# Half of the normed tokens parked in DRAM, and S5 spread one step per projection part, in a Hymba-style layer on one core

## The chip, the core and the metric

The kernel runs on one core of a Trainium2 chip. The core has a matrix engine (PE, with its weight loads PEld), a vector engine (DVE), an activation engine (ACT), a general engine (POOL) and an engine that issues DMAs (SP). Each takes its own instructions strictly in order; semaphores make one wait for another. The metric is the device time of one execution in microseconds. Before the change the median of three runs is 1477.52 us (1474.14 to 1479.11).

## The reference, cut

```python
mod = silu(c) @ w_ada + b_ada;  shift, scale, gate = split(mod, 3)
h = rmsnorm(x, norm_g) * (1 + scale) + shift          # 2048 prompt + 64 sample tokens, D = 1024
u, z_s, q, k, v, z_a, f_logit = split(h @ w_in)       # 512 columns each, 8 logits
y_ssm = Re(C scan(A, B u)) + D u                      # S5: 32 groups of 16 channels, 64 complex states
y_ssm = gelu(y_ssm);  y_ssm = y_ssm * sigmoid(y_ssm @ w_glu + b_glu) * silu(z_s)
q, k = rmsnorm per head;  logf = log_sigmoid(f_logit + b_f);  cum = cumsum(logf)
o = softmax(q k^T / 8 + cum_q - cum_k, causal) v      # 8 heads x 64; the sample also sees a cache of 512
y = x + gate * (concat(y_ssm, o * silu(z_a)) @ w_out)
```

Outputs are y, k, v, logf and the last S5 states, for the prompt and for the sample, all in float32.

## The kernel before

**Stages.** `body` (L1491) writes the program: the adaLN vectors (`Ada`, 1 MB chunks of w_ada; chunks 0 to 3 are shift and scale, 4 and 5 the gate), the projection (`InProj`) with the S5 branch (`S5`) woven into it, the GLU, attention (`Attn`) and the output projection (`Out`). A tile scheduler orders each engine's instructions ahead of time from this program and from what depends on what; at run time nothing is reordered. SP issues all DMAs, up to eight in flight.

**Projection.** The tokens are four groups of 512 (the last with the 64 sample tokens). `norm(g)` (L437) loads a group's x, transposes it on PE, applies shift and scale on ACT (hf, L460) and splits it on DVE into two float32r tiles hi and lo, so that a product takes three matmuls (`mm3`, L313: hi·whi, hi·wlo, lo·whi). The rings for hi and lo hold two groups: one half of the tokens. So the projection runs twice over the weights, for half (0, 1), then for half (2, 3). For each half there are 12 parts of 256 columns: u0, u1, then ten parts: k0, k1, v0, v1, q0, q1 and four gate parts. `weights` (L464) loads a part's 1 MB in two transfers into wst; ACT casts to whi, DVE takes the rest to wlo, in rings of 5.

`natural` (L482) makes u, v, k and q with the tokens on the partitions: a tile is 128 tokens x 256 columns, 24 matmuls. ACT evicts u and v (L500). A k or q tile goes ACT square (L507), DVE reduce (L508), DVE and POOL for the reciprocal root (L294, L295), DVE twice for the product (L511, L512). u0 also makes the forget logits (lf). `gates` (L517) makes the two gates transposed, in matmuls of 512 columns; ACT takes tanh (L534), DVE multiplies (L535), and th is stored in z_d. The tiles of the projection use three PSUM banks (2, 3, 4); two serve transposes, three S5.

**S5.** It needs u of all tokens. `setup` (L581) makes the powers of the discretised state matrix by a long chain of small DVE operations (128x32 and the like, L611). 16 steps of two groups follow. `consts(s)` (L774) makes a step's matrices on DVE (lin, btt, ca), PE and POOL; `load` (L837) brings u (un, ug); `run` (L856) does the PE matmuls us·bt, the scan on DVE (L883 to L904) and aa; `outs` (L907) does the matmuls tm·us and ca·aa, then GELU on ACT; `store` (L850) writes ys_d. A call of `s5_step` does run(s), outs(s-1) and consts(s+1), so 17 calls do all; `final` (L937) writes the states.

**Order before.** Half (0, 1): norm, u0, u1, parts; the gate chunks of w_ada ahead of part 1, setup and the first two consts ahead of part 3. Half (2, 3): norm, u0, 8 steps, u1, then parts with 3 steps after each; ahead of part 7 what is left of S5, `logf` (L538, cumulative sums of the logits) and the attention's bias. In the program:

```python
GATE_AT = 1      # w_ada chunks 4 and 5 ahead of this part of half (0, 1)
SETUP_AT = 3     # S5 setup ahead of this part of half (0, 1)
LOGF_AT = 7      # logf, bias ahead of this part of half (2, 3)
S5_STEPS = 3     # calls of s5_step after each part of half (2, 3)
```

Of the kernel before, what the change touches and what calls it, by code (L numbers as in the profile page):

```python
# [17 lines left out]
P = 128  # L18
# [25 lines left out]


GATE_AT = 1
SETUP_AT = 3
LOGF_AT = 7
S5_STEPS = 3
# [116 lines left out]
def Step(tc, a, o, ctx):  # L166
# [44 lines left out]
    cb_d = dram.tile([H, 21 * P], F32, name="cb_d")  # L211

# [187 lines left out]
class InProj:  # L400
# [62 lines left out]

    def weights(self, c0, n):  # L464
# [105 lines left out]
class S5:  # L570
# [10 lines left out]
    def setup(self):  # L581
# [5 lines left out]
        def tl(name, shape, p=sb):  # L587
            return p.tile([P] + shape, F32, name=name)
# [19 lines left out]
        S.activation(dt, dt, AF.Exp)  # L608
# [13 lines left out]
        S.activation(mag, lam, AF.Exp)  # L622
        self.r8 = tl("r8", [G], cp)
        S.activation(self.r8, lam, AF.Exp, scale=float(TC))
# [282 lines left out]
    def outs(self, s, f):  # L907
# [6 lines left out]
        for i, (c, r) in enumerate(cts):  # L914
# [11 lines left out]
            if r == P:  # L926
                S.activation(dst, py[:r].rearrange("c g (t q) -> c g t q", q=PG), AF.Gelu_apprx_tanh)
            else:
                for g in range(GS):
                    S.activation(dst[:, g], py[32 * g:32 * g + r, 0].rearrange("c (t q) -> c t q", q=PG),  # L930
                                 AF.Gelu_apprx_tanh)
# [22 lines left out]
class Attn:  # L954
# [260 lines left out]
    def scores(self, tile, kd, t):  # L1215
# [24 lines left out]
        j = i % 2 if whole and not (i == tile.nb - 1 and acc[1] is None) else 0  # L1240
# [41 lines left out]
    def run(self, out):  # L1282
# [10 lines left out]
        for i, (hp, qt) in enumerate(self.order):  # L1293
            self.cur = i
            while i not in self.ready:
# [11 lines left out]
                                   given=[False, False], n=0, nb=len(blocks), po=None)  # L1307
# [26 lines left out]
            if tile.acc[1] is not None:  # L1334
                e.PL.tensor_tensor(tile.acc[0][:, :, :nq], tile.acc[0][:, :, :nq], tile.acc[1][:, :, :nq], op=ALU.add)
# [155 lines left out]
def body(tc, a, o):  # L1491
    with ExitStack() as top:
# [35 lines left out]
        for half in ((0, 1), (2, 3)):  # L1528
            if half[0]:
                for g in half:  # L1530
                    ip.norm(g)
                ip.natural("u", 0, half)
            if half[0]:
                for _ in range(8):
                    s5_step()
            ip.natural("u", 1, half)
            for part in range(10):
                if not half[0] and part == GATE_AT:
                    for n in (4, 5):
                        ad.chunk(n)  # L1540
                if not half[0] and part == SETUP_AT:
                    s5.setup()
                    kc.update({0: s5.consts(0), 1: s5.consts(1)})
                if half[0] and part == LOGF_AT:
                    while done[0] <= NSET:
                        s5_step()
                    s5.final()
                    e.table("natural_log_exp_and_others", AF.Tanh, AF.Gelu_apprx_tanh)
                    ip.logf(s5.ps)
                    e.table("exp_and_others", AF.Exp, AF.Ln)  # L1550
                    at = Attn(e)
                    at.bias(s5.ps)
                if part < 6:
                    ip.natural("kvq"[part // 2], part % 2, half)
                else:
                    ip.gates(part - 6, half)
                if half[0]:
                    for _ in range(S5_STEPS):
                        s5_step()
# [4 lines left out]
        with ExitStack() as es:  # L1564
# [3 lines left out]
            e.table("natural_log_exp_and_others", AF.Tanh)  # L1568
# [32 lines left out]
```

## Time and profile before

| | |
|---|---|
| median of three runs | 1477.52 us |
| the profiled execution | 1474.66 us |
| its span (first to last instruction) | 1472.6 us |
| mean granted PE clock | 0.981 |
| instructions | 26341 |

By PE's matmul counts the parts end at these times (us from the start of the span):

| half | u0 | u1 | k0 | k1 | v0 | v1 | q0 | q1 | four gate parts |
|---|---|---|---|---|---|---|---|---|---|
| (0, 1) | 69.0 | 91.7 | 114.5 | 141.6 | 169.7 | 199.5 | 226.0 | 249.4 | 338.3 |
| (2, 3) | 371.9 | 410.5 | 448.8 | 496.5 | 537.8 | 578.4 | 622.7 | 665.3 | 772.7 |

The page cuts the span into 40 slices of 36.8 us; a digit is the busy share in tenths, PEclk the granted clock of PE:

```profile
PE   5899999999988999889999999999999897999998
DVE  3726886235689987996313777786886887333331
PEclk9999999999999999999999979999999999999999
```

The projection takes slices 1 to 21. In a row of the view by groups stand line, engine, operation, result and operands with their shape and count, then busy us and the mean ns of one, then the idle time before them and what ended it. In the view of PE's waits a row says who waited for whom, the us in total, how often, and the longest.

### The profile page before, as it was taken

The page shows a single profiled execution, that of the slowest core. Times are in us where ns is not written, and L with a number is a line of the kernel's source. Part 1 is how long each engine was busy: PE and PEld are TensorE (multiplying, and loading weights), DVE is VectorE, ACT ScalarE, POOL GpSimd, SP SyncE. Part 2 cuts the span into 40 slices and gives each one's busy share as a digit, 9 for nine tenths or more (in the row PEclk, how much of TensorE's full clock was granted, in tenths as well). Part 3 has the DMA queues.
Part 4 walks back from the last instruction along what each step waited for, and adds up shares of the span by engine and source line. Part 5 has one row for each costly group of instructions (what it writes and reads, how often), then busy time and mean ns, then how long its engine had stood idle before and what let it go on. Part 6 is the DMA issues. An engine that isn't in the chain of part 4 may idle for free.

```text
span 1472.6 us, 26341 instructions
## 1 busy us (share of the span) xinstructions
PE 1391.7 (95%) x9824; PEld 1092.2 (74%) x9824; DVE 912.3 (62%) x2398; ACT 538.6 (37%) x1132; POOL 485.8 (33%) x454
## 2 busy tenths in 40 slices
PE   5899999999988999889999999999999897999998
PEld 2898899889878888778899965555555454478886
DVE  3726886235689987996313777786886887333331
ACT  3722223225544444434315444445445334300000
POOL 1113253000245632561106513423423527422222
PEclk9999999999999999999999979999999999999999
DMA  9526424223233333224539533123121223054452
GB/s 339 174 88 208 108 77 130 93 93 101 79 85 92 104 96 92 61 82 130 161 111 293 178 104 120 38 75 122 47 80 31 87 64 91 20 159 146 139 150 93
DMA packets 201927, 167.11 MB, mean 113 GB/s; under 512 B 64487, under 2 KB 167619, under 8 KB 201800
## 3 DMA queue, kind: packets, MB, share of 16 engines
q1 hardware_dynamic: 201800, 165.44, 37.1%
q8 instruction: 77, 1.26, 0.4%
q14 instruction: 50, 0.41, 0.1%
HBM read 116.64 MB, written 48.76 MB: 112 GB/s over the span
## 4 chain that ended last, share of the span: by engine, by line
PE 69%; DVE 16%; issue 5%; DMA 5%; POOL 3%; ACT 1%; SPq 1%; POOLq 0%; DVEq 0%; ACTq 0%
PE low L130 29%; PE bank L130 11%; PE twin L130 11%; PE last L130 9%; PE glu L130 4%; DVE pb L1179 3%; PE bank L133 2%; PE low L133 2%; DVE acc L1253 1%; DMA un<-u_d 1%; DMA ost<-in_w_out_dram 1%; DMA wada<-in_w_ada_dram 1%; DVE lin L783 1%; DVE aa L904 1%; DVE ca L785 1%
## 5 line engine op out<-in xcount | busy, mean ns | idle before, releaser
L130 PE MATMUL low<-whi,hi 128*128 128x256 f32 (+3 forms) x1088 | 313.5, 290 | 6.3 <-DVE ev L511 5.1
L130 PE MATMUL low<-wlo,hi 128*128 128x256 f32 (+3 forms) x1088 | 310.5, 287 | 3.4 <-DVE wlo L289 3.4
L130 PE MATMUL low<-whi,lo 128*128 128x256 f32 (+3 forms) x1088 | 310.2, 288 | 0.2 <-DVE ss L294 0.2
L1179 DVE CUSTOM_DVE_ANT_0 pb<-twin,cb 128x512 bf16<-128x512 f32 (+3 forms) x328 | 200.0, 610 | 60.7 <-PE twin L130 49.5
L130 PEld LDWEIGHTS low<-whi,hi 128*128 128x128 f32 (+1 forms) x1088 | 203.3, 187 | 13.3 <-DVE ev L511 5.0
L130 PEld LDWEIGHTS low<-wlo,hi 128*128 128x128 f32 (+1 forms) x1088 | 203.5, 187 | 7.8 <-DVE wlo L289 3.8
L130 PEld LDWEIGHTS low<-whi,lo 128*128 128x128 f32 (+1 forms) x1088 | 202.7, 187 | 5.2 <-issue 3.3
L309 ACT ACTIVATE p<-twin 128x1024 f32<-128x1024 f32 (+3 forms) x180 | 149.9, 839 | 145.2 <-PE twin L130 136.7
L130 PE MATMUL bank<-p,vt 128*64 128x512 f32 (+3 forms) x704 | 142.8, 528 | 0.0
L130 PE MATMUL twin<-qs,ks 64*128 64x512 f32 (+3 forms) x1056 | 134.5, 360 | 0.0
L295 POOL TENSOR_TENSOR qss<-qss,mhalf 128x4 f32<-128x4 f32 (+1 forms) x68 | 78.5, 1155 | 132.5 <-DVE qss L294 129.7
L130 PE MATMUL low<-hi,whi 128*128 128x512 f32 (+1 forms) x320 | 113.9, 357 | 0.0
L130 PE MATMUL low<-hi,wlo 128*128 128x512 f32 (+1 forms) x320 | 113.6, 356 | 0.0
L130 PE MATMUL low<-lo,whi 128*128 128x512 f32 (+1 forms) x320 | 113.4, 355 | 0.0
L1253 DVE TENSOR_TENSOR acc<-acc,p 128x1024 f32<-128x1024 f32 (+2 forms) x88 | 86.3, 981 | 31.0 <-ACT p L309 29.4
L130 PEld LDWEIGHTS twin<-qs,ks 64*128 64x128 f32 x1056 | 95.4, 192 | 11.0
L289 DVE TENSOR_TENSOR wlo<-wst,whi 128x512 fp32r<-128x512 f32 (+1 forms) x96 | 67.2, 705 | 55.7 <-ACT whi L287 55.0
L130 PEld LDWEIGHTS bank<-p,vt 128*64 128x64 f32 x704 | 45.3, 141 | 65.3 <-issue 56.0
L130 PE MATMUL twin<-sm,kb 64*128 64x512 f32 (+3 forms) x360 | 78.0, 429 | 15.8 <-DVE pm L1179 15.3
L181 POOL TENSOR_TENSOR yo<-yo,x 128x512 f32<-128x512 f32 (+1 forms) x34 | 49.0, 1441 | 131.0 <-DVE yo L1486 126.6
L287 ACT CAST whi<-wst 128x512 fp32r<-128x512 f32 (+1 forms) x96 | 58.9, 621 | 66.4 <-DMA wst<-in_w_in_dram 48.8
L130 PE MATMUL last<-oh,mh 128*128 128x512 f32 (+1 forms) x208 | 81.4, 391 | 0.0
(362 smaller groups left out, 2783.4 us busy)
## 6 DMA issues: line engine op xcount, KB each, us to landing
wst<-in_w_in_dram SPq DMA_DIRECT2D x48, 512.0 KB
wada<-in_w_ada_dram SPq DMA_DIRECT2D x12, 1024.0 KB
cb<-cb_d SPq DMA_DIRECT2D x20, 512.0 KB
x<-in_x_prompt_dram SPq DMA_DIRECT2D x16, 512.0 KB
out_dram<-ev SPq DMA_DIRECT2D x64, 128.0 KB
x<-in_x_prompt_dram SPq DMA_DIRECT2D x32, 256.0 KB
out_dram<-yo SPq DMA_DIRECT2D x32, 256.0 KB
z_d<-th SPq DMA_DIRECT2D x24, 256.0 KB
```

Of the source, the lines that this page charges most:

```text
L130: return self.keep(self.pe.matmul(*a, **kw))
L133: return self.keep(self.pe.transpose(*a, **kw))
L181: PL.tensor_tensor(out, x, y, op=op)
L287: S.copy(hi, x)
L289: V.tensor_tensor(lo, x, hi, op=ALU.subtract)
L295: PL.tensor_tensor(out, out, bc(mhalf[:out.shape[0]], list(out.shape)), op=ALU.pow)
L309: i = S.activation(out, x, func, **kw)
L783: V.tensor_tensor(t, e.bc(p2.unsqueeze(3), shp), m2[:, gs].unsqueeze(2).to_broadcast(shp), op=ALU.mult)
L785: V.tensor_tensor(out, out, t, op=op)
L904: V.tensor_tensor(aa, aa, bb, op=ALU.add)
L1179: V.tensor_tensor_reduce(b[:, :n], ps[:, h, :n], cb[:, h, :n], 1.0, NEG, ALU.add, ALU.max, accum_out=self.pm[:, t, h, pi:pi + 1])
L1253: (PL if j else V).tensor_tensor(y[:rows, :, c0:nq], x[:rows, :, c0:nq], p[:rows, :, :n], op=ALU.add)
```

## The change

Half (0, 1) is normed first and gives only u; each of its two groups is written to DRAM in its normed, split form (`put`: four transfers of 1 MB a group, 8 MB in all, into new tensors h_d). Then half (2, 3) is normed and gives u. So u of all tokens is there before the first k part. logf and the S5 setup with the first two consts now stand between u0 and u1 of half (2, 3), and the gate chunks of w_ada ahead of norm(2). Half (2, 3) then runs its ten parts; after them `get` brings half (0, 1) back (eight transfers of 1 MB), which runs its ten. One s5_step follows each of the first 17 parts; part 17 has `final` and the bias. The number of matmuls of projection and S5 is the same.

Two smaller edits: activations of S5 go through `e.act`, which keeps their order, with the table loads written out (the page of before has seven, three of them in one group); and in the last attention tile the last six blocks are all added to acc[0], with acc[1] merged by DVE four blocks before the end, where before POOL merged the two after the last block.

```diff
-GATE_AT = 1
-SETUP_AT = 3
-LOGF_AT = 7
-S5_STEPS = 3
...
+    h_d = [[dram.tile([P, KT, 512], F32, name="h%d%d" % (g, i)) for i in range(2)] for g in range(2)]
...
+    def put(self, g):
+
+        for x, d in zip(self.h[g], self.e.h_d[g]):
+            for k in range(0, KT, 4):
+                self.e.nc.sync.dma_start(d[:, k:k + 4], x.bitcast(F32)[:, k:k + 4, :512])
+
+    def get(self, g):
+        self.h[g] = tuple(self.ht.tile([P, KT, 576], F32R, tag=t, name=t) for t in ("hi", "lo"))
+        for k in range(0, KT, 4):
+            for x, d in zip(self.h[g], self.e.h_d[g]):
+                self.e.nc.sync.dma_start(x.bitcast(F32)[:, k:k + 4, :512], d[:, k:k + 4])
...
-        S.activation(dt, dt, AF.Exp)
+        e.act(dt, dt, AF.Exp)
...
+        e.table("trig_and_small", AF.Exp, AF.Ln)
         sn = tl("sn", [G])
-        S.activation(sn, ang, AF.Sin)
+        e.act(sn, ang, AF.Sin)
         hs = tl("hs", [G])
-        S.activation(hs, ang, AF.Sin, scale=0.5)
+        e.act(hs, ang, AF.Sin, scale=0.5)
+        e.table("gelu_apprx_tanh_and_others", AF.Sin)
...
-        j = i % 2 if whole and not (i == tile.nb - 1 and acc[1] is None) else 0
+        late = tile.end and i >= tile.nb - 6
+        j = i % 2 if whole and not late else 0
+        if late and i == tile.nb - 4:
+            V.tensor_tensor(acc[0], acc[0], acc[1], op=ALU.add)
...
-            if tile.acc[1] is not None:
+            if tile.acc[1] is not None and not tile.end:
                 e.PL.tensor_tensor(tile.acc[0][:, :, :nq], tile.acc[0][:, :, :nq], tile.acc[1][:, :, :nq], op=ALU.add)
...
         for g in range(2):
             ip.norm(g)
+            ip.put(g)
         ip.natural("u", 0, (0, 1), w)
+        ip.natural("u", 1, (0, 1))
+        for n in (4, 5):
+            ad.chunk(n)
         e.masks()
-        kc = {}
+        for g in (2, 3):
+            ip.norm(g)
+        ip.natural("u", 0, (2, 3))
+        e.table("natural_log_exp_and_others", AF.Tanh)
+        ip.logf(s5.ps)
+        s5.setup()
+        kc = {0: s5.consts(0), 1: s5.consts(1)}
...
-        for half in ((0, 1), (2, 3)):
-            if half[0]:
+        ip.natural("u", 1, (2, 3))
+        at = None
+        for half in ((2, 3), (0, 1)):
+            if not half[0]:
                 for g in half:
-                    ip.norm(g)
-                ip.natural("u", 0, half)
-            if half[0]:
-                for _ in range(8):
-                    s5_step()
-            ip.natural("u", 1, half)
+                    ip.get(g)
             for part in range(10):
...
-                if half[0]:
-                    for _ in range(S5_STEPS):
-                        s5_step()
+                if done[0] <= NSET:
+                    s5_step()
+                elif not at:
+                    s5.final()
+                    at = Attn(e)
+                    at.bias(s5.ps)
```

In the rows that follow, line numbers of the new program differ by a few: L124 is the matmul (L130 before), L127 the transpose (L133), L478 the load of wst (L471), L515, L518 and L519 the k and q eviction (L508, L511, L512), L618 the setup's DVE operation (L611), L543 the store of z_d, L463 put and L469 get.

**DVE at the first tiles of a k part.** Before, at k0 of half (0, 1) the evictions stand by themselves, with the wlo of the next weights between them, and the setup's first operations follow at the last k tile:

```order
L508 TENSOR_REDUCE qss_2_1047<-ev_2_549 128x4
L294 TENSOR_SCALAR qss_2_1047<-qss_2_1047 128x4
L289 TENSOR_TENSOR wlo_2_214<-wst_0_199,whi_2_213 128x2x256
L289 TENSOR_TENSOR wlo_3_218<-wst_1_210,whi_3_217 128x2x256
L511 TENSOR_TENSOR ev_2_549<-low_124,qss_2_1047 128x256
```

Now, at k0 of half (2, 3):

```order
L618 TENSOR_TENSOR wre_0_1568<-wre_0_1568,wt_166848_0_1684 128x32
L518 TENSOR_TENSOR ev_2_561<-low_132,qss_0_2225 128x256
L622 TENSOR_SCALAR wim_0_1569<-wim_0_1569 128x32
L515 TENSOR_REDUCE qss_2_2289<-ev_0_505 128x4
L618 TENSOR_TENSOR ta_119936_0_1566<-ta_119936_0_1566,cm_157248_0_1540 128x32
L618 TENSOR_TENSOR ta_122112_0_1567<-ta_122112_0_1567,cn_157504_0_1541 128x32
L618 TENSOR_TENSOR un_166976_0_1690<-wre_0_1568 128x32
L518 TENSOR_TENSOR ev_3_589<-low_136,qss_1_2257 128x256
```

The chain of the setup stands ahead of the k evictions and between them, where before it stood beside v. Counted from the last operation on the logits of u0, 208 DVE instructions stand ahead of the first k eviction.

**PE between two projection tiles.** us,bt are a run's matmuls, tm,us and ca,aa those of an outs, the others with whi and wlo are projection. Before, in a part of half (2, 3), the work of two steps stands within one tile:

```order
L130 MATMUL low_132<-whi_0_202,lo_0_302 128x256
L130 MATMUL bank_73<-us_0_3851,bt_0_2113 128x264
L130 MATMUL low_132<-whi_0_202,hi_0_301 128x256
L130 MATMUL low_132<-wlo_0_203,hi_0_301 128x256
L130 MATMUL low_132<-whi_0_202,lo_0_302 128x256
L130 MATMUL bank_69<-tm_1_2166,us_1_3905 128x128
L130 MATMUL low_132<-whi_1_206,hi_0_301 128x256
L130 MATMUL low_116<-ca_0_2115,bp_0_2120 32x128 x2
L130 MATMUL bank_69<-ca_1_2152,aa_1_3906 128x128
```

Now, in a gate part of half (2, 3), at the step from one group to the other:

```order
L124 MATMUL bank_77<-tm_0_1899,us_0_2496 128x128
L124 MATMUL bank_77<-ca_0_1883,aa_0_2497 128x128
L124 MATMUL low_132<-hi_0_305,whi_3_221 128x512
L124 MATMUL low_132<-lo_0_306,whi_3_221 128x512
L124 MATMUL low_132<-hi_0_305,wlo_3_222 128x512
```

A step's work now stands between matmuls of twice the length. Counted over the whole order, some 7.4 of the 17 steps' work stands in v and gate parts, 5.1 in q parts, 2 in the k parts that follow the setup and 3.6 in the k parts that follow the get (counted by PE's S5 instructions, each part of a step by its share).

**SP at the switch of halves.** Between the gate stores (z_d) and S5's transfers (ys_d, un, kd_d, tm) of the first half's end now stand the eight loads of 1 MB:

```order
L543 DMA z_d<-th_0_4420 128x512
L469 DMA hi_0_305<-h_66 128x4x512
L469 DMA lo_0_306<-h_67 128x4x512
L863 DMA ys_d<-un_196608_1_3181 1024x1x64
L863 DMA ys_d<-un_135424_1_3185 64x1x64
L469 DMA lo_0_306<-h_67 128x4x512
L469 DMA hi_0_305<-h_66 128x4x512
L543 DMA z_d<-th_1_4448 128x512
L823 DMA kd_d<-kd_0_1893 64x240
```

Before, at the switch, x is loaded (4 MB in rows of 128x1024) between stores of q:

```order
L428 DMA x_0_137<-in_x_prompt_dram 128x1024
L515 DMA q_d<-ev_2_549 128x256
L428 DMA x_1_145<-in_x_prompt_dram 128x1024
L515 DMA q_d<-ev_3_577 128x256
```

In the new order the other four loads of get (hi_1, lo_1) stand some ten rows later, and the first two transfers of put (2 MB) stand between the third and the fourth x load of norm(1). What moved: 8 MB of loads now stand among gate stores, and 8 MB of stores among the x loads of the front.

More of the change, by code (lines that the diff above doesn't have):

```diff
@@ L621, in setup @@
         mag = tl("mag", [G])
-        S.activation(mag, lam, AF.Exp)
+        e.act(mag, lam, AF.Exp)
         self.r8 = tl("r8", [G], cp)
-        S.activation(self.r8, lam, AF.Exp, scale=float(TC))
+        e.act(self.r8, lam, AF.Exp, scale=float(TC))
         ang = tl("ang", [G])
@@ L926, in outs @@
             if r == P:
-                S.activation(dst, py[:r].rearrange("c g (t q) -> c g t q", q=PG), AF.Gelu_apprx_tanh)
+                e.act(dst, py[:r].rearrange("c g (t q) -> c g t q", q=PG), AF.Gelu_apprx_tanh)
             else:
                 for g in range(GS):
-                    S.activation(dst[:, g], py[32 * g:32 * g + r, 0].rearrange("c (t q) -> c t q", q=PG),
-                                 AF.Gelu_apprx_tanh)
+                    e.act(dst[:, g], py[32 * g:32 * g + r, 0].rearrange("c (t q) -> c t q", q=PG), AF.Gelu_apprx_tanh)
         for j, tab in enumerate((co, si)):
@@ L1306, in run @@
             tile = SimpleNamespace(hp=hp, qt=qt, nq=nq, nz=nz, z=z, q=self.q[i] + (self.ready[i],), acc=[None, None],
-                                   given=[False, False], n=0, nb=len(blocks), po=None)
+                                   given=[False, False], n=0, nb=len(blocks), po=None, end=i == len(self.order) - 1)
             for u in range(0, len(blocks), PVG):
@@ L1526, in s5_step @@
                     kc[s + 1] = s5.consts(s + 1)
-        for half in ((0, 1), (2, 3)):
-            if half[0]:
+        ip.natural("u", 1, (2, 3))
+        at = None
+        for half in ((2, 3), (0, 1)):
+            if not half[0]:
                 for g in half:
-                    ip.norm(g)
-                ip.natural("u", 0, half)
-            if half[0]:
-                for _ in range(8):
-                    s5_step()
-            ip.natural("u", 1, half)
-            for part in range(10):
[L1538 to L1545, printed above, removed]
-                        s5_step()
[L1547 to L1552, printed above, removed]
+                    ip.get(g)
+            for part in range(10):
                 if part < 6:
@@ L1556, in body @@
                     ip.gates(part - 6, half)
-                if half[0]:
-                    for _ in range(S5_STEPS):
-                        s5_step()
+                if done[0] <= NSET:
[4 more added lines that the diff above has]
+                    at.bias(s5.ps)
         out = Out(e)
@@ L1567, in body @@
                 at.glu(Glu(e, e.banks(es2, "glu", 2)))
-            e.table("natural_log_exp_and_others", AF.Tanh)
+            e.table("natural_log_exp_and_others", AF.Tanh, AF.Gelu_apprx_tanh)
             at.twins += e.banks(es, "twin", 1, 1024)
```

## The prediction, made before the change was timed

> **What bounds the kernel now.** I read the page's first two sections, then a table of busy time by stretch, then PE's waits and the groups of instructions in the stretches that the change touches.
>
> ```profile
> PE 1391.7 (95%) x9824; PEld 1092.2 (74%) x9824; DVE 912.3 (62%) x2398; ACT 538.6 (37%) x1132; POOL 485.8 (33%) x454
> ...
> PE 69%; DVE 16%; issue 5%; DMA 5%; POOL 3%; ACT 1%; SPq 1%; POOLq 0%; DVEq 0%; ACTq 0%
> ```
>
> PE is busy 95% of the 1472.6 us, and the chain that ended last lies on it for 69%. The change takes no matmul away, so it can only win where PE stands or runs slowly. The 16% on DVE says who makes it wait. I cut the projection, 30 to 773 us, at the ends of its parts (columns: stretch; length; busy us of PE, PEld, DVE, ACT and POOL with records; granted clock; DMA share; GB/s):
>
> ```profile
> 30.00:69.00 39.00, 33.61 (x264) 29.66 (x261) 25.67 (x64) 28.14 (x59) 6.27 (x11) 1.00 0.60 202
> 69.00:142.00 73.00, 73.00 (x602) 69.44 (x601) 31.98 (x82) 18.35 (x42) 15.93 (x16) 1.00 0.44 136
> 142.00:199.50 57.50, 54.60 (x418) 50.50 (x417) 50.38 (x256) 14.76 (x32) 11.93 (x20) 0.94 0.44 116
> ...
> 372.00:410.50 38.50, 35.01 (x280) 32.45 (x279) 26.32 (x56) 20.84 (x61) 13.76 (x14) 1.00 0.25 72
> 410.50:496.60 86.10, 77.84 (x608) 70.70 (x606) 78.81 (x212) 37.83 (x121) 46.09 (x53) 0.98 0.31 83
> 496.60:578.50 81.90, 76.25 (x598) 69.26 (x597) 65.87 (x153) 38.15 (x119) 31.43 (x39) 0.98 0.36 98
> 578.50:665.40 86.90, 77.09 (x596) 69.71 (x595) 77.63 (x205) 38.17 (x121) 47.69 (x54) 0.98 0.31 86
> 665.40:725.20 59.80, 59.80 (x393) 52.78 (x392) 31.88 (x106) 25.98 (x60) 7.28 (x10) 1.00 0.47 133
> 725.20:772.90 47.70, 47.70 (x291) 43.52 (x290) 10.22 (x17) 9.74 (x18) 6.22 (x4) 1.00 0.42 135
> ```
>
> PE has gaps in two zones only: where nearly all S5 steps lie (372 to 665: u1, k, v, q of the second half of the tokens), and where the S5 setup lies (142 to 199.5: v of the first half). Gates (last two rows) leave DVE idle more than half the time. In the S5 zone PE waits for DVE results:
>
> ```profile
> PE low L130 <- DVE ca L785: 5.4, 3, 2.1
> PE low L130 <- DVE ev L511: 5.1, 7, 1.4
> PE low L133 <- DVE btt L785: 3.2, 4, 1.5
> PE bank L130 <- ACT un L927: 2.7, 2, 1.7
> PE low L130 <- DVE aa L904: 2.6, 1, 2.6
> ```
>
> Some are S5's own (ca, btt, aa), some the q and k eviction (ev).
>
> **The steps spread out.** How many steps lie in 372 to 665? A run issues four matmuls us,bt, an outs eight large ones ca,aa:
>
> ```profile
> L130 PE MATMUL bank<-ca,aa 128*128 128x128 f32 x76 | 16.3, 300 | 2.6 <-DVE aa L904 2.4
> L130 PE MATMUL bank<-us,bt 128*128 128x264 f32 x40 | 13.0, 406 | 2.7 <-ACT un L927 1.7 <-ACT us L870 1.0
> L130 PE MATMUL low<-ca,aa 128*128 128x128 f32 x36 | 8.0, 306 | 2.6 <-DVE aa L904 2.6
> L130 PE MATMUL low<-us,bt 128*128 128x264 f32 x20 | 6.2, 392 | 0.0
> ```
>
> (40+20)/4 = 15 runs and (76+36)/8 = 14 outs: 14.5 steps. The seven parts without S5 are 7 x 216 = 1512 matmuls of 256 columns. In a stretch of nothing else one takes 25.00/214 = 117 ns:
>
> ```profile
> 75.00:100.00 25.00, 25.00 (x214) 25.00 (x213) 4.91 (x11) 5.86 (x13) 1.94 (x2) 1.00 0.29 91
> ```
>
> That is 177 of the 293.4 us, so a step costs (293.4 - 177)/14.5 = 8.0 us here. Of this PE stands 3.5 + 8.3 + 5.7 + 9.8 = 27.2 us, and the clock of 0.98 costs 2% of 254.9 = 5.1: 32.3/14.5 = **2.2 us a step** that a place with a free DVE gives back. The gates confirm it: 59.8 - 47.7 = 12.1 us for about 1.7 steps (two outs, one run) with the logit and bias work among it, and no gap: 7.1 a step at most, against 8.0, and 5.8 by the gaps and the clock.
>
> Afterwards, by the order on PE, about 7.4 steps lie in v and gate parts, 5.1 in q parts, and 4.5 in k parts. DVE's side: its busy time of the four S5 rows is 26.3 + 78.8 + 65.9 + 77.6 = 248.6 us. The tiles and weights come from these rows:
>
> ```profile
> L511 DVE TENSOR_TENSOR ev<-low,qss 128x256 f32<-128x256 f32 x32 | 13.4, 420 | 7.4 <-POOL qss L295 7.0
> L508 DVE TENSOR_REDUCE qss<-ev 128x4 f32<-128x256 f32 x32 | 13.1, 409 | 1.2 <-ACT ev L507 1.2
> ...
> L512 DVE TENSOR_TENSOR ev<-ev,kg 128x256 f32<-128x256 f32 x16 | 8.8, 555 | 0.0
> ...
> L294 DVE TENSOR_SCALAR qss<-qss 128x4 f32<-128x4 f32 x32 | 6.6, 207 | 0.1
> ...
> L289 DVE TENSOR_TENSOR wlo<-wst,whi 128x512 fp32r<-128x512 f32 x8 | 5.5, 685 | 0.4 <-ACT whi L287 0.4
> ```
>
> A q or k tile is 0.42 + 0.41 + 0.5 + 0.2 = 1.5 us of DVE, a part's four wlo 2.8. 36 tiles and 28 wlo are 74 of the 248.6, so a step is about 12 us of DVE. Two v and two q parts with one step each are 27 + 11 + 48 = 86 us of DVE beside 4 x (25.3 + 5.8) = 124 of PE, 70%; it was 95% (257.4 of 272.8 us in 390 to 690). So I give v and gate parts the whole 2.2 us, 7.4 x 2.2 = 16, and q parts half, 5.1 x 1.1 = 6. In the k parts of the half that comes last, 16 x 1.5 + 5.6 + 3.6 x 12 = 73 us of DVE stand beside some 68 of PE: nothing is won; nor in the other k parts, which the setup holds. Sum **-22 us**, bounds -32 (all 14.5) and 0 (the latency of a step's own chain, not DVE's load, makes the gaps).
>
> **The setup moved ahead of k.** It lay beside v, whose tiles ACT evicts. It cost 57.5 - 54.6 = 2.9 us of gaps and 6% of 57.5 = 3.5 of clock there, 6.4 in all. Afterwards DVE has 208 instructions between u0's last logit operation and the first k eviction, and 256 took 50.4 us there: 0.197 each, 41 us. PE has meanwhile u1 (28 us) and three tiles of k0 (8.5), 37 us; then its PSUM banks for tiles are full and it waits. Up to the last eviction of k1 it is some 102 us of DVE against 85 of PE: +17, less the 6.4 that go, **+10.5 us**. Bounds: +3 where DVE gets a start on it during u0 and its short operations overlap, +18 where the log gates and the chain of dependent small operations stretch it. I take the middle, what the counts give.
>
> **The halves parked in DRAM.** 8 MB go out at the front, in eight transfers of 1 MB, two of them ahead of an x load, and come back at the switch of halves. The trace has no store of this kind. The nearest rows:
>
> ```profile
> 0.00:25.00 25.00, 11.19 (x46) 3.24 (x47) 6.88 (x26) 7.30 (x12) 4.77 (x24) 1.00 0.93 320
> 50.00:75.00 25.00, 24.79 (x202) 24.02 (x202) 16.99 (x39) 17.86 (x40) 3.67 (x6) 1.00 0.58 191
> ```
>
> 320 GB/s with the queue full: 1 MB is 3.3 us, 4 MB 13, 8 MB 26. From 50 to 75 the queue has 42% free, so the 2 MB ahead of x (6.6 us) are partly covered by u's matmuls: **+4**, bounds 0 and +8 (all 2 MB, and a little behind). At the switch, a group can come in (4 MB, 13 us) once the last gate part is done with the group whose place it takes. Beside it PE has the other group's 48 matmuls, which take 25.00/109 = 229 ns each in gates:
>
> ```profile
> 275.00:300.00 25.00, 25.00 (x109) 20.26 (x108) 5.85 (x9) 4.96 (x9) 0.00 (x0) 1.00 0.29 95
> ```
>
> 11 us, and some steps' matmuls: **+2**, bounds 0 and +8. Gate stores and S5's transfers queue on SP behind these megabytes, which is a rival below.
>
> A rule of the Trainium skill speaks against this. Page "DMA: Bandwidth & Descriptors", section "Queues, rings and completion order": all DMAs issued by SP use one ring on each of the 16 engines and are taken up in ring order, so a small transfer gets its turn behind megabytes issued earlier. In the trace there is this row for small S5 loads behind 512 KB weight loads:
>
> ```profile
> L846 DVE COPY ug<-un 128x512 f32<-128x512 f32 x14 | 7.1, 508 | 7.8 <-DMA un<-u_d 7.8
> ```
>
> 7.8 us of DVE waiting over 14 loads says little is lost now; by the rule the get would add up to its own 26 us to what stands behind, instead of my +2.
>
> **The rest.** Activation tables go from 7 loads to 5:
>
> ```profile
> L300 ACT ACT_TABLE_LOAD x3 | 3.8, 1283 | 0.1
> ```
>
> 2 x 1.3 us on an engine at 37%: 0, bounds -2.6 and 0. In the last attention tile a POOL addition of 2.4 us goes and DVE takes one 128x1024 addition more; there PE already runs the output projection's matmuls beside it: 0, bounds -2 and +1 (DVE's acc takes 0.98 us).
>
> **Sum**, against the profiled execution (1474.7, of which 1472.6 is span): -22 + 10.5 + 4 + 2 = -5.5, so 1469.2. The median of the three runs, 1477.5, lies 2.9 above the profiled one; carried over: **1472 us**.
>
> **The rivals.**
> - *The setup is absorbed.* The 41 us start under u0 and the k evictions never wait; k also gains. Speaking for it: PE's 73.0 of 73.0 us with k parts at DVE 32 of 73. Then the +10.5 falls to -6 at best, and the sum is about -18: 1460, or 1452 with the larger saving.
> - *The big transfers block what SP issues behind them* (the skill's rule above). For 13 to 26 us from the switch on, gate stores (z_d), S5's un, tm and the next weights stand behind 8 MB; th's two buffers fill, the gate evictions stop, PE with them, and the S5 chain of the first k part starts late on a DVE already at 73 of 68 us. It decides once the transfers outlast the last gate group's 11 to 13 us: 26 - 12 = +14, and at the front the same for x_3: +4 more. Sum about +13 to +15, **1490**; with the setup's upper bound 1498. Against it: before, DMA share is 0.31 to 0.36 here, and weights are a part ahead.
> - *The steps don't get cheaper.* Gaps come from a step's chain of waits on un, ca, btt, not from DVE's load. Then -22 is 0 and the sum +16.5, 1494. Against it: gates show 0 gaps with steps.
>
> **How the numbers follow.** Forecast 0.48 (1462 to 1484), absorbed setup 0.18 (1452 to 1462), blocked row 0.26 (1484 to 1500), steps not cheaper 0.08. 0.3%, about what a measurement of this kernel can tell from no change, is 4.4 us. Forecast splits into 0.24 under 1473.1, 0.19 between, 0.05 above 1481.9. Faster 0.24 + 0.18 = 0.42; same 0.19 + 0.02 (a mild block) = 0.21; slower 0.37. The range, 1452 to 1500, holds all cases but the tails.
>
> **What would show it.** In the profile after: PE without gaps and a clock of 1.00 in v, q and gate parts (spread right); PE waiting for DVE ev and wlo in the first k parts (setup); PE waiting for the DMAs of hi and lo at the switch, or DVE for un (get); the first 75 us longer by x waits (put). It is wrong if k parts show no waits, or if the gaps in v parts keep their size with one step each.

## The result, and the profile after

The changed kernel takes 1459.14 us, median of four runs (1458.15 to 1462.94), against 1477.26 beside it: ratio 0.9884, with a 95% interval of 0.9859 to 0.9909. That is 17 to 18 us faster. The prediction said 1472, within 1452 to 1500. The profiled execution took 1458.38 us, its span is 1456.7, 15.9 shorter than before. A repeat (x11_again, in the experiments) gave 0.9867.

The whole gain lies in the projection. It ends at 756.9 us where it ended at 772.7; from there to the end it is 699.9 us before and 699.8 after, so the edits of the last attention tile and of the table loads (five on the page after, seven before) changed nothing that shows. By PE's matmul counts the parts end at (us; before in the first two columns, by half):

| part | before (0, 1) | before (2, 3) | after (0, 1) | after (2, 3) |
|---|---|---|---|---|
| u0 | 69.0 | 371.9 | 71.6 | 142.1 |
| u1 | 91.7 | 410.5 | 100.6 | 172.4 |
| k1 | 141.6 | 496.5 | 550.0 | 235.8 |
| v1 | 199.5 | 578.4 | 599.1 | 297.9 |
| q1 | 249.4 | 665.3 | 659.0 | 366.2 |
| last gate part | 338.3 | 772.7 | 756.9 | 480.6 |

The first section of the page after, and the lines by engine of the second:

```profile
PE 1387.7 (95%) x9824; PEld 1091.4 (75%) x9824; DVE 911.2 (63%) x2400; ACT 540.2 (37%) x1130; POOL 482.0 (33%) x452
...
PE   6899989999999999999999999999999898999998
DVE  2656999567677785665214777885886877342331
```

DVE does the same work (911 us), but the run of sevens to nines in slices 12 to 18 is gone. Nines now stand in slices 5 to 7, where the setup meets k, and fives to eights from there to slice 19. The busy time by stretch, cut at the ends of parts of the kernel after (columns as in the prediction): the rest of u0, u1, u0 of the other half, u1, k0, k1, then v to q, gates, and of half (0, 1) k, v to q and the first two gate parts.

```profile
30.00:71.60 41.60, 36.21 (x268) 32.42 (x268) 23.54 (x57) 26.36 (x54) 4.24 (x7) 0.92 0.82 286
71.60:100.60 29.00, 27.15 (x215) 26.44 (x214) 13.04 (x29) 15.42 (x34) 2.85 (x5) 0.94 0.80 274
100.60:142.10 41.50, 41.50 (x311) 33.67 (x309) 25.95 (x74) 23.42 (x53) 4.29 (x12) 1.00 0.65 205
142.10:172.40 30.30, 28.32 (x241) 27.88 (x239) 29.21 (x163) 10.40 (x24) 8.18 (x10) 1.00 0.53 116
172.40:201.00 28.60, 25.86 (x219) 25.68 (x217) 26.42 (x131) 5.92 (x14) 11.47 (x16) 1.00 0.21 63
201.00:235.80 34.80, 31.45 (x249) 29.04 (x248) 33.94 (x100) 14.51 (x48) 24.65 (x33) 1.00 0.27 78
235.80:366.20 130.40, 125.54 (x1034) 119.68 (x1033) 91.05 (x227) 50.47 (x148) 54.97 (x58) 1.00 0.32 91
366.20:480.60 114.40, 114.01 (x720) 100.50 (x719) 78.69 (x166) 45.50 (x126) 29.53 (x38) 1.00 0.46 137
480.60:550.00 69.40, 65.35 (x517) 60.61 (x516) 62.25 (x167) 32.41 (x99) 36.17 (x41) 0.98 0.45 145
550.00:659.00 109.00, 107.69 (x885) 104.00 (x884) 67.27 (x173) 40.20 (x110) 32.16 (x39) 0.98 0.36 102
659.00:709.60 50.60, 50.60 (x247) 41.08 (x246) 20.10 (x55) 15.70 (x36) 5.71 (x7) 1.00 0.43 130
```

Three things are to be seen. In v and q of half (2, 3) DVE is busy 91 of 130 us, 70%, and PE's gaps are 4.9 us; before, in the same parts with more of S5 in them, they were 5.7 + 9.8 = 15.5 of 168.8 us. In u1, k0 and k1 (142 to 235.8) DVE is busy 89.6 of 93.7 us: the setup. And from 30 to 100.6 us PE has gaps and a lower clock, and the DMA engines are busy 80% of the time; the run with one store, below, shows how much of this is the stores.

PE's waits between 142 and 240 us in the kernel after:

```profile
PE low L124 <- DVE ev L518: 3.3, 4, 2.5
PE low L124 <- DVE wim L622: 2.7, 1, 2.7
PE low L124 <- DVE cm L573: 2.0, 1, 2.0
```

The k evictions (L518) and the setup's chain (L622) are there as forecast, and logf (L573), which was not; but all are small. At the switch of halves, 480 to 521 us:

```profile
PE low L124 <- DVE ev L518: 3.1, 2, 2.6
PE bank L124 <- DVE aa L913: 0.7, 1, 0.7
PE low L127 <- DVE btt L794: 0.2, 1, 0.2
```

No row names the loads of hi and lo, nor S5's un.

**What a step costs, place by place.** PE's records beyond the projection's own count S5's work, and the time beyond the projection's own (117 ns for a matmul of 256 columns; gates by the last two gate parts of before, 47.7 us, or 22.2 a part of half (0, 1)) is its price. Before, 372 to 665.4: 116.5 us for 2082 - 1512 = 570 records, 204 ns each; 14.5 steps are 39.3 records a step, so 8.0 us.

| stretch after | S5 records | time beyond the projection | ns a record | us a step |
|---|---|---|---|---|
| v, q of (2, 3) | 1034 - 864 = 170 | 130.4 - 101.1 = 29.3 | 172 | 6.8 |
| gates of (2, 3) | 720 - 576 = 144 | 114.4 - 95.4 = 19.0 | 132 | 5.2 |
| k of (0, 1), with the get | 517 - 384 = 133 | 69.4 - 44.9 = 24.5 | 184 | 7.2 |
| v, q of (0, 1) | 885 - 768 = 117 | 109.0 - 89.9 = 19.1 | 163 | 6.4 |
| two gate parts of (0, 1) | 247 - 192 = 55 | 50.6 - 44.4 = 6.2 | 113 | 4.4 |

Together 98 us for 619 records, 158 ns: **6.2 us a step, against 8.0**. (The three parts with the setup, left out here, hold 61 records more.) A step is dearest where DVE is busiest (k: 62 of 69 us) and cheapest beside gates. With PE's gaps and what the lower clock takes subtracted, an estimate from these rows, a record costs 148 ns before and 129 to 144 in the first four rows of the table. So most of what a step saves is time in which PE stood or ran slowly.

### The profile page after: what moved, and what is told of

Same layout as the page of the kernel before. It is cut to its first block, busy times and chain, and to the rows that moved or that the text cites. A ratio compares the mean times of both kernels' runs of the same rounds, so it can differ in the third digit from the quotient of the medians.

```text
span 1456.7 us, 26343 instructions
## 1 busy us (share of the span) xinstructions
PE 1387.7 (95%) x9824; PEld 1091.4 (75%) x9824; DVE 911.2 (63%) x2400; ACT 540.2 (37%) x1130; POOL 482.0 (33%) x452
## 4 chain that ended last, share of the span: by engine, by line
PE 62%; DVE 14%; issue 11%; POOL 6%; DMA 5%; ACT 1%; SPq 0%; POOLq 0%; DVEq 0%; ACTq 0%
PE low L124 30%; PE twin L124 12%; PE bank L124 10%; PE glu L124 4%; POOL yo L175 3%; PE bank L127 3%; DVE pb L1187 2%; PE low L127 2%; PE last L124 2%; DMA x<-in_x_prompt_dram 1%; DVE acc L1264 1%; POOL qss L290 1%; DMA ost<-in_w_out_dram 1%; DMA wst<-in_w_in_dram 1%; POOL ol L175 1%
## 5 line engine op out<-in xcount | busy, mean ns | idle before, releaser
L124 PE MATMUL low<-whi,hi 128*128 128x256 f32 (+3 forms) x1088 | 313.4, 290 | 14.5 <-DVE ev L518 9.0
L124 PE MATMUL low<-wlo,hi 128*128 128x256 f32 (+3 forms) x1088 | 309.5, 286 | 0.0
L124 PE MATMUL low<-whi,lo 128*128 128x256 f32 (+3 forms) x1088 | 308.3, 286 | 0.0
L124 PEld LDWEIGHTS low<-whi,hi 128*128 128x128 f32 (+1 forms) x1088 | 204.5, 188 | 19.7 <-issue 10.5
L124 PEld LDWEIGHTS low<-whi,lo 128*128 128x128 f32 (+1 forms) x1088 | 203.5, 188 | 3.9 <-issue 3.0
L124 PEld LDWEIGHTS low<-wlo,hi 128*128 128x128 f32 (+1 forms) x1088 | 204.6, 188 | 2.0 <-issue 1.7
L124 PE MATMUL bank<-p,vt 128*64 128x512 f32 (+3 forms) x704 | 142.8, 528 | 0.0
L124 PE MATMUL twin<-qs,ks 64*128 64x512 f32 (+3 forms) x1056 | 134.6, 361 | 0.0
L290 POOL TENSOR_TENSOR qss<-qss,mhalf 128x4 f32<-128x4 f32 (+1 forms) x68 | 82.1, 1207 | 132.6 <-DVE qss L289 129.1
L124 PE MATMUL low<-hi,whi 128*128 128x512 f32 (+1 forms) x320 | 114.3, 357 | 0.0
L124 PE MATMUL low<-lo,whi 128*128 128x512 f32 (+1 forms) x320 | 114.0, 356 | 0.0
L124 PE MATMUL low<-hi,wlo 128*128 128x512 f32 (+1 forms) x320 | 114.0, 356 | 0.0
L1264 DVE TENSOR_TENSOR acc<-acc,p 128x1024 f32<-128x1024 f32 (+4 forms) x89 | 87.6, 984 | 28.6 <-ACT p L304 27.0
L124 PEld LDWEIGHTS twin<-qs,ks 64*128 64x128 f32 x1056 | 95.2, 192 | 11.2
L124 PEld LDWEIGHTS bank<-p,vt 128*64 128x64 f32 x704 | 45.1, 140 | 65.8 <-issue 56.2
L124 PE MATMUL twin<-sm,kb 64*128 64x512 f32 (+3 forms) x360 | 77.8, 428 | 15.4 <-DVE pm L1187 15.1
L124 PE MATMUL last<-oh,mh 128*128 128x512 f32 (+1 forms) x208 | 81.3, 391 | 0.0
L124 PE MATMUL last<-ol,mh 128*128 128x512 f32 (+1 forms) x208 | 81.1, 390 | 0.0
```

The costliest lines, as they stand in the source:

```text
L124: return self.keep(self.pe.matmul(*a, **kw))
L290: PL.tensor_tensor(out, out, bc(mhalf[:out.shape[0]], list(out.shape)), op=ALU.pow)
L1264: (PL if j else V).tensor_tensor(y[:rows, :, c0:nq], x[:rows, :, c0:nq], p[:rows, :, :n], op=ALU.add)
```

## The experiments

All start from the changed kernel unless said otherwise. The time after the projection differs by up to 11 us from one profiled execution to the next with the code unchanged (the last section has it), so the ends of parts tell more here than the total; both are given.

**The get left out.**

```diff
-                    ip.get(g)
+                    ip.h[g] = ip.h[g + 2]
```

> The changed kernel without the eight loads at the switch of halves: the ten parts of half (0, 1) use the normed tokens of half (2, 3) that are still in SBUF, so the outputs of half (0, 1) are not the reference's. The put stays. Changed kernel: 1459.1. Theory of the prediction (the get costs PE about 2 us, at most the 4.1 us of gaps and 4% of clock that k0 of half (0, 1) shows, 5.6 us in all): 1453 to 1458. Rival (the 8 MB hold up everything SP issues behind them, 13 us and more): 1446 or less. If the get is hidden altogether: 1459.

1463.1 us, 0.9894 (0.9868 to 0.9920): the total lies above all that was expected, even above the 1459 of a get that is hidden altogether. In the profiled execution the part behind the projection took 707.9 us, against 699.8. From the end of half (2, 3) to the end of the projection it takes 273.2 us. Five executions with the get (the changed kernel twice, x2, x7, x9) take 276.3, 276.2, 273.3, 274.6 and 274.8, mean 275.0. By this the get costs 1.8 us, near the 2 of the prediction's sum; but it is one execution against five that scatter by 3 us. The rival's 13 us are not there. The switch itself gains more, 31.9 us for k0 against 39.8, but some of S5's work moved behind it (251 records in k0 against 274), and k1 to v1 took 6.3 us more.

**One store in place of eight.** The get reads that 1 MB eight times.

```diff
-                self.e.nc.sync.dma_start(d[:, k:k + 4], x.bitcast(F32)[:, k:k + 4, :512])
+        if g == 0:
+            self.e.nc.sync.dma_start(self.e.h_d, self.h[g][0].bitcast(F32)[:, :4, :512])
```

> The changed kernel with one store of 1 MB in place of eight; the get reads that 1 MB eight times, as many bytes as before, so the outputs of half (0, 1) are not the reference's. Theory of the prediction (put costs 4 us, between 0 and 8): 1451 to 1457, most likely 1455. What the trace after suggests (gaps of 7.2 us plus 5 us of lower clock up to 101 us, against 5.4 us in the same stretch before, so up to 7 us): 1452. Rival (the stores are hidden, the front is longer for the order of norm and u): 1459.

1459.2 us, 0.9867 (0.9841 to 0.9894); the projection ends at 748.9. Its front, cut at its own parts:

```profile
30.00:70.60 40.60, 35.17 (x271) 31.81 (x268) 25.25 (x61) 28.61 (x60) 5.79 (x9) 0.96 0.68 225
70.60:94.20 23.60, 23.60 (x202) 23.60 (x201) 10.33 (x22) 11.76 (x27) 1.76 (x3) 1.00 0.44 143
```

u1 loses its gaps and its clock dip, 23.6 us instead of 29.0. u0 of half (2, 3) ends at 136.3; in seven executions whose front is as in the change (the changed kernel, x1, x3, x4, x9, x10, x11) it ends at 139.2 to 142.1, mean 140.4. By this the stores cost 4.1 us, the forecast's figure. The total, 1459.2, is the rival's 1459; but the part behind the projection took 707.1 us in the profiled execution, so the total can't decide it.

**S5 packed again.** Three calls of s5_step after a part until they are done.

```diff
-                    s5_step()
+                    for _ in range(3):
+                        s5_step()
```

> The changed kernel with three calls of s5_step after each part until they are done, in place of one, so that most of S5 stands in the ten parts of half (2, 3) and none after k1 of half (0, 1). Nothing else. Theory of the prediction (a step costs up to 2.2 us more where DVE is loaded; a dozen steps move from free places to loaded ones): 1470 to 1481. Rival (a step's price is its own chain and does not depend on the place; the gain of the change comes from elsewhere): 1455 to 1463.

1473.4 us, 0.9965 (0.9946 to 0.9984); the projection ends at 773.2, 16.3 later, within what the theory gave. v to q of half (2, 3):

```profile
236.40:406.00 169.60, 154.30 (x1194) 140.00 (x1192) 144.95 (x353) 75.49 (x239) 83.83 (x93) 0.97 0.32 87
```

(169.6 - 101.1) us for 1194 - 864 = 330 records are 208 ns, 8.2 us a step: the price of before, in the same parts where one step a part costs 6.8. DVE is busy 145 of 170 us. So packing the steps brings the price back. With it the whole gain in the projection goes, and by the totals some 14 of the 18 us. What this run does not separate is the load of DVE from the room that a step leaves to the next. PE's waits in v to q, with three calls a part (the longest four of seven rows) and then in the changed kernel:

```profile
PE low L124 <- DVE ev L518: 5.5, 5, 2.1
PE low L127 <- DVE btt L794: 3.1, 4, 1.3
PE low L124 <- ACT un L304: 1.9, 2, 1.5
PE bank L124 <- ACT us L879: 1.4, 1, 1.4
```

```profile
PE low L124 <- DVE ev L518: 2.5, 3, 1.0
PE low L124 <- ACT us L879: 1.3, 1, 1.3
PE low L124 <- DVE ca L794: 0.8, 2, 0.6
PE bank L124 <- DVE aa L913: 0.2, 1, 0.2
```

The waits for evictions (ev) are 5.5 us against 2.5; those for S5's own values (btt, un, us, ca, aa, ws) are 9.5 against 2.3. Packed steps make PE wait above all for S5 itself.

**Two calls a part within half (2, 3), no parking.** From the kernel before:

```diff
-LOGF_AT = 7
-S5_STEPS = 3
+LOGF_AT = 8
+S5_STEPS = 2
...
-                for _ in range(8):
+                for _ in range(1):
```

> The kernel before with S5 spread inside its half (2, 3) alone: one call of s5_step after u0 in place of eight, two after each part in place of three, logf and bias ahead of part 8 in place of 7. No parking in DRAM. Before: 1477.8, projection ends at 772.7 us in its profile. Theory that the gain comes from spreading over all parts with a free DVE (two steps and a q or k part are 24 + 16 us of DVE beside 25 + 12 of PE, so those parts stay loaded; only some four steps reach gates): 1466 to 1473, projection ends at 761 to 768. Rival (spreading inside the half is all that counts, the parking is not needed): 1458 to 1462.

1493.2 us, 1.0097 (1.0076 to 1.0118): slower, which neither side expected; the projection ends at 783.4 where it ended at 772.7. k0 to q1, the next gate parts, and the stretch with logf and the bias:

```profile
398.40:641.50 243.10, 219.38 (x1724) 200.20 (x1723) 194.26 (x494) 104.58 (x318) 106.91 (x124) 0.99 0.31 84
641.50:708.30 66.80, 65.05 (x413) 55.71 (x412) 54.12 (x127) 30.76 (x92) 22.57 (x30) 1.00 0.36 100
708.30:758.30 50.00, 39.64 (x237) 34.33 (x237) 23.78 (x88) 18.26 (x44) 6.24 (x9) 0.83 0.42 113
```

A step in k0 to q1 is no cheaper: 243.1 - 1296 x 0.117 = 91.5 us for 428 records, 214 ns. 71 records a part instead of 81 leave DVE at 194 of PE's 219 us. The loss comes at the end: logf and the bias now stand behind the last step with two gate parts left, PE stands 10.4 of 50 us there and runs at 0.83. That alone is about the 10.7 us by which the projection ends later. So two steps a part cost what three did; but the run does not show that the parking is needed, since an earlier logf, which was not tried, might have ended the projection sooner than before.

**v ahead of k.** The setup then stands beside v.

```diff
-                    ip.natural("kvq"[part // 2], part % 2, half)
+                    ip.natural("vkq"[part // 2], part % 2, half)
```

> The changed kernel with the parts in the order v, k, q in place of k, v, q, in both halves: the setup chain on DVE then stands beside v parts, whose tiles ACT evicts. Theory of the prediction (the collision of the setup with the k evictions costs 10.5 us net): 1447 to 1451. What the trace after suggests (8 us of PE gaps from u1 to k1, part of which is S5's first steps): 1453 to 1457. Rival (DVE is the bound of the whole stretch whatever the order, so the wait only moves to the k parts behind): 1459.

1455.4 us, 0.9844 (0.9819 to 0.9869); the projection ends at 750.1. The first two parts take 55.0 us instead of 63.4, and the next two 69.4 instead of 62.1: u1 to the sixth part is 222.3 us, in the changed kernel 224.1. In half (0, 1) the same: 58.6 instead of 69.4, then 62.6 instead of 49.1. Most of what the first two give back, the next two take. The time lies in the 1453 to 1457 of the second guess, but not for its reason: u1 to the sixth part gains 1.8 us and not 8. Of the mechanisms the rival's is the nearer one.

**q behind k.** If v behind k takes up DVE's lag, q there should not.

```diff
-                    ip.natural("kvq"[part // 2], part % 2, half)
+                    ip.natural(("kqv" if half[0] else "kvq")[part // 2], part % 2, half)
```

> The changed kernel with the parts of half (2, 3) in the order k, q, v in place of k, v, q; half (0, 1) as in the change. In the changed kernel DVE is 11 us behind PE when PE ends k1 (last eviction at 246.6, PE at 235.8), and the two v parts behind it take the lag up, since ACT evicts their tiles. Theory (this is why the setup cost 1 us net and not 10.5): with q behind k the lag stays and PE waits in q; from u1 to the sixth part PE takes 5 to 10 us longer than the 224 us of the changed kernel, and the projection ends 4 to 10 us later than 756.9. Rival (the setup costs little since its operations are shorter than counted, wherever it stands): within 2 us of 224 and 756.9.

1460.0 us, 0.9866 (0.9848 to 0.9885); u1 to the sixth part 221.7 us, the projection ends at 753.5. My theory falls: q0 behind k takes 39.5 us with 3.7 of gaps, where v0 there took 31.1 with 1.1; but v at the end takes 27.0 and 28.0 with none. Over the stretch the order hardly matters; the rival's 2 us are just missed, on the early side.

**The setup ahead of norm(2).**

```diff
+        e.table("natural_log_exp_and_others", AF.Tanh)
+        s5.setup()
+        kc = {0: s5.consts(0), 1: s5.consts(1)}
         for g in (2, 3):
             ip.norm(g)
         ip.natural("u", 0, (2, 3))
-        e.table("natural_log_exp_and_others", AF.Tanh)
+        e.table("natural_log_exp_and_others", AF.Sin)
         ip.logf(s5.ps)
-        s5.setup()
-        kc = {0: s5.consts(0), 1: s5.consts(1)}
+        e.table("gelu_apprx_tanh_and_others", AF.Ln)
```

> The changed kernel with the S5 setup and the first two consts written ahead of norm(2), one activation table load more before and after logf; all else the same. Changed kernel: 1459.1, projection ends at 756.9 in its profile, u1 to k1 take 93.7 us. Theory of the prediction (the setup chain holds the k evictions, 10.5 us net): u1 to k1 take 84 to 87 us and the projection ends 5 to 9 us earlier, at 748 to 752. Rival (DVE is loaded in the whole front, so the setup's 40 us are paid by the norm of groups 2 and 3 instead): u0 to u1 grows by what k0 and k1 give back, the end stays within 2 us of 756.9.

1533.9 us, 1.0365 (1.0342 to 1.0387): a plain miss of both. The stretch from 140 to 180 us, and then PE's longest waits from 90 to 230:

```profile
140.00:180.00 40.00, 1.96 (x8) 0.79 (x8) 39.00 (x182) 1.52 (x11) 15.11 (x29) 0.50 0.00 0
```

```profile
PE low L124 <- DVE ca L794: 23.6, 1, 23.6
PE low L127 <- DVE un L618: 23.0, 1, 23.0
PE low L124 <- DMA wada<-in_w_ada_dram: 13.7, 4, 6.9
```

PE has 2 us of work in 40. Its own order now has transposes and matmuls of setup and consts (the rows of un and ca) ahead of what u0 still needs of norm(2), and these wait 23.0 and 23.6 us for the chain on DVE. u0 of half (2, 3) ends at 224 instead of 142. u1 and k0 to k1 give back only 3.5 us (90.2 against 93.7). So it is the place beside u1 and k0, where PE has projection matmuls to run meanwhile, that keeps the chain nearly free.

**Both puts behind both norms.**

```diff
         for g in range(2):
             ip.norm(g)
+        for g in range(2):
             ip.put(g)
```

> The changed kernel with both puts written after both norms, so that all x loads of norm(1) go ahead of the first store. Same bytes. In the changed kernel u1 of the first half ends at 97.5 to 100.6 us and u0 of the second at 139.2 to 142.1; with one store of eight at 94.2 and 136.3. Theory of the prediction (2 MB ahead of an x load are what the put costs): u0 of the second half ends at 136 to 138, the projection 2 to 5 us earlier. Rival (bandwidth: 8 MB of stores lie in the same stretch as 4 MB of x and the weights, whichever goes first): it ends at 139 to 142 as before.

1461.6 us, 0.9887 (0.9868 to 0.9905); u0 of half (2, 3) ends at 139.6, within the 139.2 to 142.1 of the unchanged front, and the projection at 755.2. The order against norm(1)'s x is not what the stores cost; that it is the bandwidth fits (286 GB/s from 30 to 71.6 us in the changed kernel, 225 with one store), but wasn't tried by itself.

**All three together.**

> The changed kernel with all three: parts in the order v, k, q, setup ahead of norm(2), puts after both norms. If the three gains add up as the theory of the prediction has them: projection ends at 740 to 746, 1444 to 1450. If setup and part order give the same gain twice (one collision, removed by either): 747 to 752, 1451 to 1455.

1531.1 us, 1.0380 (1.0351 to 1.0409): the early setup spoils it, as alone. It says nothing on the sum of the others.

**Parts interleaved**, v0, k0, gate, v1, k1, gate, q0, gate, q1, gate.

```diff
-                if part < 6:
-                    ip.natural("kvq"[part // 2], part % 2, half)
-                else:
-                    ip.gates(part - 6, half)
+                kind, i = (("v", 0), ("k", 0), ("g", 0), ("v", 1), ("k", 1), ("g", 1), ("q", 0), ("g", 2),
+                           ("q", 1), ("g", 3))[part]
+                if kind != "g":
+                    ip.natural(kind, i, half)
+                else:
+                    ip.gates(i, half)
```

> The changed kernel with the parts of each half in the order v0, k0, gate, v1, k1, gate, q0, gate, q1, gate, so that a part that loads DVE is followed by one that does not. Same work. In the changed kernel PE still has 18.7 us of gaps between 142 and 756, in v first 14. Theory (what is left is lag of DVE behind k and q parts): projection ends at 742 to 750, 1449 to 1455. Rival (what is left is the start of the setup and the wait for the switch, which the order of later parts does not change): 750 to 757, as v first or the changed kernel.

1455.0 us, 0.9831 (0.9810 to 0.9852). From the end of u0 to the last part it takes 612.1 us, v first 610.4, the changed kernel 614.8: 2.7 us less, and v first 4.4. The time is at the edge of the theory's range, but the projection ends at 753.2, in the rival's. What is left is mostly not DVE's lag behind k and q. Both beat the change by some 4 to 5 us by their medians, though the intervals of the ratios overlap.

**The changed kernel again.**

> The changed kernel once more, unchanged, beside these on one chip: 1458 to 1462, projection ends at 755 to 758.

1460.0 us, 0.9867 (0.9846 to 0.9888); the projection ends at 754.9.

**Two PSUM banks for the tiles in place of three.**

```diff
-        self.ps = Banks(e.psum, 2, 3, 4)
+        self.ps = Banks(e.psum, 2, 3)
```

> The changed kernel with two PSUM banks for the projection's tiles in place of three; the scheduler then puts more of the first S5 steps beside k0 and k1. In the changed kernel PE ends k1 10.8 us before the last k eviction (235.8 against 246.6), so the lag of DVE behind the setup reached PE only less these 10.8 us. Theory (the slack is the tiles that fit in the banks, about 3 us each, and what the prediction's +17 left out): PE ends k1 only 6 to 8 us ahead of the last k eviction, and its gaps from u1 to k1 rise from 8.1 to 11 us or more. Rival (the lead comes from something else, the banks don't set it): the lead stays at 10 to 11 us and the gaps at 8.

1519.3 us, 1.0271 (1.0233 to 1.0309). PE ends k1 at 273.3, the last k eviction starts at 279.7: 6.4 us of lead where three banks gave 10.8. The tiles can be counted: behind PE's end of k1 two k evictions are still to start (275.6 and 279.7), with three banks it was three (238.1, 242.5 and 246.6). u1, k0 and k1:

```profile
144.00:176.70 32.70, 29.87 (x240) 29.42 (x239) 30.99 (x167) 10.41 (x24) 7.42 (x10) 0.95 0.53 114
176.70:223.60 46.90, 34.40 (x239) 31.82 (x238) 42.42 (x170) 9.62 (x32) 22.79 (x36) 0.89 0.18 52
223.60:273.30 49.70, 42.41 (x319) 37.86 (x318) 48.63 (x125) 24.43 (x78) 31.16 (x31) 0.97 0.26 70
```

22.6 us of gaps against 8.1. The lead is as the theory gave it; the gaps are more, but this kernel also has more of S5 beside k (798 records in the three parts against 709), so not all of them are the bank's. The projection ends at 830.4, 73.5 us later than in the changed kernel, about half of it by the end of k1: the third bank is worth more than this lead.

## Why the prediction came out as it did

The direction and the main mechanism were right, and the time lies in the range; the point was 13 us too slow, and the time lies outside the 1462 to 1484 that the forecast gave itself. Against the profiled execution the sum was -5.5 us, and it is -15.9 in the span.

- **The steps: -22 forecast.** The table's 619 records are 15.7 steps, 98 us. Before, 14.5 of them took 116.5 us and 1.2 more at the 7.1 of the gates 8.5, 125 in all: -27 (at the 4.7 that the 102 S5 records of that row give, -24). What is left of the span's -15.9 after the other three terms is -15.9 - 1.7 - 4.1 - 1.8 = -23.5, a remainder and no measurement of its own. By either the term held, a little small. By place: gates were given 2.2 us a step and gained 2.8, k was given nothing and gained 0.8; v and q, given 2.2 and 1.1, gained 1.2 and 1.6 (the two rows of the table). The counts of steps by place, in the section on the change, add up to 18.1 instead of 17.
- **What makes a step cheaper.** The bound of 0 is out: x3 brings the price back to 8.2 us by packing alone. Its reason, a step's own chain, is not out: x3's waits are above all for S5's own values. Nor does the load of DVE alone, the prediction's reason, put the prices in order: with one step a part the k parts cost 7.2, the get's price in it, where DVE is busy 95% of PE's time (62 of 65 us); with two a part x5 cost 8.4 at 89%. Whether the load or the room between steps makes the price stays open; no run changed one without the other.
- **The get: +2 forecast, 1.8 measured. The put: +4 forecast, 4.1 measured** (x1, x2). Within a front that scatters by 3 us this is closer than the method deserves; in part it is luck. The reason given for the put, 2 MB ahead of an x load, was not it (x7).
- **The setup: +10.5 forecast, +1.7 found. This is the step that failed,** in size. Its counts held: from the last logit operation (143.3) to the first k eviction (183.4) it is 40 us, 41 forecast; to the last eviction of k1 (246.6) it is 103, 102 forecast. The error is what was done with them. The prediction took "some 102 us of DVE against 85 of PE: +17", as if PE had to wait for the last eviction. PE was done with k1 at 235.8, 10.8 us ahead of it, because three tiles fit into its banks (at that time three k tiles were still to be evicted); the prediction counted that lead where the first eviction comes, and left it out at the end. Some 3 us of it are there without the setup too: before, the last k eviction of half (0, 1) starts at 145.0, and PE ends k1 at 141.6. With the lead taken off, 17 - 10.8 = 6.2 are left. PE's gaps in u1, k0 and k1 are 2.0 + 2.7 + 3.4 = 8.1 us, logf's 2.0 among them, so 6.1 for the setup; all 8.1 less the 6.4 us that go at the old place are 1.7. x12 shows that the lead shrinks with the banks (two tiles and 6.4 us with two). That v parts behind k take up the lag was my next idea, and x9 contradicts it: with q there PE waits 2.6 us more in that part, and gets it back later.
- **The carry to the median: +2.9 forecast.** The median after lies 0.8 above its profiled execution. The changed kernel did not have the offset that the three runs of before had; 2 of the 13 us are this.
- Tables and the last attention tile: 0 forecast; 699.8 us after the projection against 699.9.

So 1472 - 8.8 (setup) - 2.1 (offset) = 1461, and the steps' -23.5 in place of -22 is most of the 2 us that are left. Since the -23.5 is a remainder, this sum closes by itself and proves nothing.

By the time, the rival that came is the absorbed setup (1452 to 1462), which had 0.18. By its mechanism it came in part: it has the k evictions never wait and the term at -6, where PE waits for them and for the chain, and the term is +1.7. Its "about -18" is also not what its terms give: -22 - 6.4 + 4 + 2 = -22.4, which is 1455. The blocked queue didn't come. The Trainium skill's page "DMA: Bandwidth & Descriptors", section "Queues, rings and completion order", speaks of ring order on the DMA engines; if small transfers queued behind the get's megabytes here, no wait of PE in the rows at the switch came of it, and x1 puts the price of the whole get at some 2 us.

## What to carry to other kernels

Work beside a stream costs by how it is spread over it. Here a step of S5 cost 8 us where two or three calls stood in a part, 6.4 to 7.2 with one call beside v, q and k, and about 5 beside the long matmuls of the gates. So a detour of 16 MB through DRAM that cost some 6 us, and made those places reachable, paid for itself about four times over. When two engines' times over a stretch are compared, the lead that the buffers allow has to be taken off at the stretch's end, not only at its start. And a long chain of small operations, with the matmuls that hang on it, belongs behind what the bound engine can run meanwhile, not ahead of it (x6, +75 us), however free its engine looks on average.

## What was not expected of the hardware

The rest of the kernel after the projection, with the same instructions but for the edit of the last attention tile, took 699.9, 699.8, 707.9, 707.1, 696.9 and 700.1 us in six profiled executions (before, after, x1, x2, x3, x4). Two stretches of 50 us at its start, of the changed kernel and then of x1_no_get:

```profile
756.90:806.90 50.00, 48.14 (x402) 45.17 (x400) 20.02 (x57) 27.11 (x59) 31.12 (x27) 0.97 0.91 276
806.90:856.90 50.00, 48.37 (x399) 39.80 (x396) 38.27 (x117) 19.67 (x43) 14.78 (x15) 0.83 0.46 139
```

```profile
755.10:805.10 50.00, 46.93 (x402) 43.78 (x401) 20.43 (x57) 27.15 (x59) 31.06 (x27) 1.00 0.90 275
805.10:855.10 50.00, 49.67 (x375) 41.41 (x375) 35.28 (x110) 18.93 (x42) 14.79 (x15) 0.76 0.47 138
```

The granted clock is 0.83 in the one and 0.76 in the other, and PE is 24 matmuls behind at the end of the second stretch. In all the traces the clock has two values, 1.00 and 0.50, and half clock comes in stretches of 3.41 us or a multiple of it (the last one is cut by the end): here 17.1 us from 834.5 in the changed kernel and 23.9 us from 830.3 in x1. After the projection it adds up to 38 us in the one and 52 in the other. At half clock PE loses half the time, so this is some 7 of the 8.1 us between them, half a per cent of the total. The stretches of one execution start on one grid: in the changed kernel at 39.1, 90.3, 517.0, 619.4, 762.8 and 834.5 us, which lie 15, 125, 30, 42 and 21 times 3.413 us apart. Against the kernel's start the grid lies elsewhere in each execution, which may be why the same instructions get 17.1 us or 23.9; no run tests this. In x6, with PE nearly idle for 40 us, the clock is 0.50 throughout. That agrees with the page "TensorE: Matmul & The Clock Gate", section "Part 1: The HAM clock gate", of the Trainium skill, by which half the clock is the state of an idle PE and the window that decides runs freely; the grid is what the traces show of the window.
